# A hybrid attention and retention layer on one core: the last product as seven block products in a stage of its own, after both branches multiplied tile by tile

## The chip, the core and the metric

The kernel runs on one core of one Trainium2 chip. The metric is the device time of one execution in microseconds. Names used below: TensorE (PE, matmuls), its weight loads (PEld), VectorE (DVE), ScalarE (ACT), GpSimd (POOL), and SyncE (SP), the queue that issues every DMA of this kernel. PSUM is the memory that matmuls write their results to; a bank of it here holds a tile of 128 x 512.

## What is computed

One layer for 2048 frames of a new stream (the prompt) and 64 frames of running streams (the samples), with 1024 channels. Of the reference, cut to its end:

```
h = rmsnorm(x, norm_g) @ w_in        # one projection, split into columns
qa, ka, va, za, qb, kb, vb, zb, ga, gb = jnp.split(h, ...)
oa = diff_attention(qa, ka, va, ...) # branch A, 512 channels out
ob = retention(qb, kb, vb, ...)      # branch B, 512 channels out
...
def layer_output(x, oa, ob, za, zb, ga, gb, subln_g, lam_init, w_oa, w_ob, w_out):
    oa = (rmsnorm(oa, subln_g) * (1.0 - lam_init)).reshape(B, T, W_A) * jax.nn.silu(za)
    ob = rmsnorm(ob).reshape(B, T, W_B) * jax.nn.silu(zb)
    m = ga * (oa @ w_oa) + gb * (ob @ w_ob)
    return x + m @ w_out
```

`ga` and `gb` are sigmoids (with a bias per channel); `w_oa` and `w_ob` (in the kernel `w_o_diff` and `w_o_ret`) are 512 x 1024, `w_out` is 1024 x 1024. The change concerns `layer_output`. Everything is float32.

## The kernel before

**Products in parts.** Every float32 product is made of three matmuls on a high part (a cast by ACT) and a low part (the rest, mostly by DVE) of each operand: high by high, high by low, low by high. So each tile of an operand costs a cast and a subtraction before TensorE can use it.

**Order.** The program is written by tasks with priorities that a planner resumes one after the other along an estimated clock. A task takes a room in memory by `take` and hands it back by `give`; the number of rooms of each kind stands in `BUFS`. The order of TensorE, ACT and DVE is what the tasks write; SyncE's and POOL's orders are made from it afterwards by a scheduler. Each of these orders is fixed when the program is built: an instruction that waits holds back all that stand behind it on its engine.

**The closing stage.** The stages before it (projection, attention, retention) leave in DRAM the branch outputs `oaT`, `obT`, the raw gates of the branches `zaT`, `zbT` and the raw merge gates `gaT`, `gbT`, channels by tokens. `out_stream` (L1798) then goes through 8 groups of 264 columns, 256 tokens of the prompt and 8 of the samples each. For one group:

- `og_fin` (L1625) makes the eight operands of the branches (four per branch, 128 channels each): it loads `on` and `z`, multiplies on POOL (L1628), takes a sigmoid on ACT (L1631), multiplies on DVE (L1634), casts (L1642) and subtracts (L1645). The rooms for `on` and `z` are called "oz", those of the operands "og".
- `m_tile` (L1667) makes one tile of the merged product, 128 of the 1024 channels (`ct` counts them): for each branch four blocks of three matmuls 128x264 (L1685 to L1687) into a PSUM bank, `mm` for branch A and `s` for branch B, two banks of each. 192 matmuls for the eight tiles of a group.
- `gate` loads the two raw gates of the tile into rooms "gt" (8 of them) and takes the sigmoid (L1656); `m_fin` (L1696) multiplies each gate with its bank on DVE (L1704), adds the two on POOL (L1708), casts (L1714), subtracts (L1717), and copies the sample columns aside (`ms`, L1723).
- `y_tile` (L1727) multiplies 128 of the group's tokens with `w_out`: two halves of 512 channels, each 8 x 3 matmuls 128x512 (L1758 to L1760) into a bank `at`; `y_fin` adds x on DVE (L1791) and stores. Two of these per group, 96 matmuls. In the last group the tile of the 64 sample frames (L1752 to L1754, 32 matmuls) stands between the two.

So the branch product and the last product alternate, group by group. `load_wo` and `load_wout` load the weights and split them (`split_fin`). Loads are issued at L138, stores at L143, all on SyncE.

Of the kernel before, what the change touches and what calls it, by code (L numbers as in the profile page):

```python
# [35 lines left out]
        "oz": 11, "og": 16, "gt": 8, "wst": 4, "m": 16, "xt": 2, "yt": 2}  # L36
# [8 lines left out]
EARLY = 3  # L45
# [17 lines left out]
class Hybrid:  # L63
    def __init__(self, tc, ins, outs):
        self.tc = tc
        self.nc = tc.nc
        self.i = ins
        self.o = outs
        self.pe = self.act = self.dve = self.pool = self.dma = 0.0
        self.tasks = []  # L70
        self.seq = 0
        self.res = {k: Res(n) for k, n in BUFS.items()}
        self.res["row"] = Res(ROWS)
        self.live = {"z": 0, "w": 0, "r": 0}
        self.done = set()
# [79 lines left out]
    def scratch(self):  # L155
# [13 lines left out]
        self.obT = tc.dram_tile([4, 128, 8 * GW], F32, name="obT")  # L169

    def consts(self):
# [33 lines left out]
        nc.vector.tensor_scalar_mul(self.gsub, self.gsub, 0.8)  # L205
# [1201 lines left out]
    def ret_block(self, k, t0, r, first):  # L1407
# [88 lines left out]
        nc.vector.tensor_scalar(ms, ms, 1.0 / 128, EPS, op0=ALU.mult, op1=ALU.add)  # L1496
# [69 lines left out]
    def load_wo(self, q):  # L1566
        sl = slice(256 * q, 256 * q + 256)
        for br, name in enumerate(("w_o_diff", "w_o_ret")):
            for kt in range(4):
                h, l, slot = self.wo[br][kt]  # L1570
                yield from self.take("oz")
                s = self.sb(self.z3, [128, GW], "oz", "wst")[:, :256]
                t = self.ld(s, self.i[name][0, 128 * kt:128 * kt + 128, sl], 1 << 17)
                self.spawn(self.split_fin("oz", h[:, sl], l[:, sl], s, t, (kt + q) % 3 == 0, slot, q), 2)
                yield self.pe

    def load_wout(self):
        pool = self.z4
        for ct in range(8):
            h = pool.tile([128, 1024], F32R, tag=f"woh{ct}", name=f"woh{ct}")  # L1580
            l = pool.tile([128, 1024], F32R, tag=f"wol{ct}", name=f"wol{ct}")
            self.wout.append((h, l, {}))
        for nh in range(2):
            sl = slice(512 * nh, 512 * nh + 512)
            for ct in range(8):
                h, l, slot = self.wout[ct]
                k = 8 * nh + ct
                tag = ("xt", "xt", "yt", "yt")[k] if k < 4 else "wst"
                yield from self.take(tag)
                s = self.sb(pool, [128, 512], tag, "wst")  # L1590
                t = self.ld(s, self.i["w_out"][0, 128 * ct:128 * ct + 128, sl], 1 << 18)
                self.spawn(self.split_fin(tag, h[:, sl], l[:, sl], s, t + 600, False, slot, nh), 2)
                self.wout_left -= 1
                yield self.pe

    def out_prep(self):
        pa = self.z3
        for br, name in enumerate(("w_o_diff", "w_o_ret")):
            for kt in range(4):
                h, l = (pa.tile([128, 1024], F32R, tag=f"{name}{n}{kt}", name=f"{name}{n}{kt}") for n in "hl")  # L1600
                self.wo[br].append((h, l, {}))
        yield from self.load_wo(0)
        for g in range(8):
            gsl = slice(GW * g, GW * g + GW)
            for br, (oT, zT) in enumerate(((self.oaT, self.zaT), (self.obT, self.zbT))):
                for kt in range(4):
# [7 lines left out]
                    self.spawn(self.og_fin(on, z, t, og), 1)  # L1614
                    yield self.pe
            if g == 0:
                for ct in range(EARLY):
                    yield from self.take("oz", 2)
                    pair = [self.sb(pa, [128, GW], "oz", "gt") for _ in range(2)]
                    self.spawn(self.gate(ct, pair, "oz"), 1)  # L1620
                for q in range(1, 4):
                    yield from self.load_wo(q)
                yield lambda: self.wout_left == 0

    def og_fin(self, on, z, t, og):  # L1625
        nc = self.nc
        yield t
        nc.gpsimd.tensor_mul(on, on, z)  # L1628
        t = self.G(GW, self.pe)
        yield t  # L1630
        nc.scalar.activation(z, z, AF.Sigmoid)  # L1631
        t = self.A(GW, t)
        yield t
        nc.vector.tensor_mul(on, on, z)  # L1634
        t = self.V(GW + 100, t)
        self.give("oz", t)
        yield from self.take("og", 2)
        h = self.sb(self.z3, [128, GW], "og", "ogh", F32R)
        l = self.sb(self.z3, [128, GW], "og", "ogl", F32R)
# [10 lines left out]
    def gate(self, n, pair, tag):  # L1650
        g, ct = divmod(n, 8)
        for br, gT in enumerate((self.gaT, self.gbT)):
            t = self.ld(pair[br], gT[ct][:, GW * g:GW * g + GW], 1 << 17)
        yield t
        for br in range(2):
            self.nc.scalar.activation(pair[br], pair[br], AF.Sigmoid, bias=self.bg[:, br, ct:ct + 1])  # L1656
            t = self.A(GW, t, 123)
        self.gts[n] = (pair, t, tag)

    def gate_prep(self):  # L1660
        for n in range(EARLY, 64):
            yield from self.take("gt", 2)
            pair = [self.sb(self.z4, [128, GW], "gt") for _ in range(2)]
            self.spawn(self.gate(n, pair, "gt"), 0)
            yield self.pe

    def m_tile(self, g, ct, og):  # L1667
        nc = self.nc
        csl = slice(128 * ct, 128 * ct + 128)
        pss = []  # L1670
        for br, tag in ((0, "mm"), (1, "s")):
            yield from self.take(tag)
            ps = self.psum(tag)[:, :GW]
            for kt in range(4):
                wh, wl, tw = self.wo[br][kt]
# [336 lines left out]
```

## Time and profile before

| what | us |
|---|---|
| median of 3 runs (lowest, highest) | 1969.37 (1968.32, 1969.64) |
| profiled execution, its span | 1970.5 |
| TensorE busy from 1200 to 1588 us, of 388.0 | 388.0 |
| TensorE busy from 1588 us to the end, of 382.5 | 376.6 |
| DVE, ACT, POOL busy in the same 382.5 | 179.0, 129.1, 100.0 |
| branch matmuls of the first group: first start, then the first start of the second group | 1588.42, 1635.92 |

The profiled execution is one more run, taken with the profiler; its span is 1.1 us above the median of the timed ones. The profile gives the busy time of each engine, the idle time before each group of instructions with what ended it, and the start of each instruction. Matmuls overlap in their pipeline, so a row's duration is longer than the distance to the next start. From 1588 us on, the program is in the closing stage; DVE is busy for 47% of it, ACT for 34%, POOL for 26%.

### The profile page before, as it was taken

How to read it: one execution, taken by the hardware profiler on the slowest of the kernel's cores; microseconds unless marked ns; L12 is line 12 of the kernel's file. 1: busy time of each engine (PE TensorE's matmuls, PEld its weight loads, DVE VectorE, ACT ScalarE, POOL GpSimd, SP SyncE). 2: the span in 40 equal slices, each digit the busy share in tenths (PEclk: the TensorE clock that was granted, in tenths of full speed). 3: DMA queues.
4: the chain of work that ended last, by engine and by line, in shares of the span. 5: the costliest groups of instructions: out<-in, count | busy, mean ns of one | idle time of the engine just before them, and what ended most of it. 6: DMA issues, size and time to landing. Idle time of an engine off the chain costs nothing. (4 is left out here: it accounts for less than half of the span.)

```text
span 1970.5 us, 34013 instructions
## 1 busy us (share of the span) xinstructions
PE 1954.8 (99%) x12158; PEld 1753.9 (89%) x12158; DVE 1048.8 (53%) x2795; ACT 993.2 (50%) x2190; POOL 418.9 (21%) x387
## 2 busy tenths in 40 slices
PE   9999999999999999999999999999999999999999
PEld 7878999999988989999998888888888888888997
DVE  6553665536555236547757656635753356444433
ACT  6432776655544436436756666635654554333321
POOL 2310211212111121212112112112112434222210
PEclk9999999999999999999999999999999999999999
DMA  7647554336655656664352342553234666444432
GB/s 245 212 129 195 152 158 122 110 89 164 180 162 166 163 158 194 189 198 148 105 144 92 97 134 78 160 148 97 65 94 130 197 215 205 145 134 136 140 94 60
DMA packets 332429, 286.03 MB, mean 145 GB/s; under 512 B 65250, under 2 KB 296930, under 8 KB 332259
## 3 DMA queue, kind: packets, MB, share of 16 engines
q1 hardware_dynamic: 332258, 283.85, 49.0%
q8 instruction: 96, 1.57, 0.4%
q14 instruction: 75, 0.61, 0.1%
HBM read 187.22 MB, written 91.49 MB: 141 GB/s over the span
## 5 line engine op out<-in xcount | busy, mean ns | idle before, releaser
L516 PE MATMUL mm<-xh,wh 128*128 128x512 f32 (+2 forms) x1280 | 459.1, 359 | 0.0
L516 PE MATMUL mm<-xh,wl 128*128 128x512 f32 (+2 forms) x1280 | 452.3, 353 | 0.0
L516 PE MATMUL mm<-xl,wh 128*128 128x512 f32 (+2 forms) x1280 | 451.7, 353 | 0.0
L480 POOL TENSOR_TENSOR wl<-ws,wh 128x512 fp32r<-128x512 f32 x189 | 257.0, 1372 | 814.9 <-ACT wh L470 629.5
L516 PEld LDWEIGHTS mm<-xh,wl 128*128 128x128 f32 x1280 | 241.0, 188 | 31.6
L516 PEld LDWEIGHTS mm<-xh,wh 128*128 128x128 f32 x1280 | 241.3, 189 | 29.0 <-issue 0.2
L516 PEld LDWEIGHTS mm<-xl,wh 128*128 128x128 f32 x1280 | 241.6, 189 | 27.9
L516 PE MATMUL mm<-wh,xh 128*128 128x256 f32 (+1 forms) x824 | 258.4, 314 | 1.2 <-DVE tlo L753 1.0
L516 PE MATMUL mm<-wh,xl 128*128 128x256 f32 (+1 forms) x824 | 253.4, 308 | 0.0
L516 PE MATMUL mm<-wl,xh 128*128 128x256 f32 (+1 forms) x824 | 253.1, 307 | 0.1
L1119 DVE TENSOR_TENSOR atl<-at,ath 128x512 fp32r<-128x512 f32 (+1 forms) x144 | 93.8, 660 | 162.6 <-ACT ath L1117 162.6
L810 ACT COPY ev<-mm 128x512 f32<-128x512 f32 x140 | 71.5, 511 | 194.1 <-PE mm L516 166.0
L516 PEld LDWEIGHTS mm<-wh,xh 128*128 128x128 f32 x824 | 156.7, 190 | 10.9 <-DVE tlo L753 1.4
L516 PEld LDWEIGHTS mm<-wl,xh 128*128 128x128 f32 x824 | 156.9, 190 | 9.2 <-POOL wl L480 0.3
L516 PEld LDWEIGHTS mm<-wh,xl 128*128 128x128 f32 x824 | 156.7, 190 | 8.0
L1035 ACT ACTIVATE row<-row,a_mx 128x1024 f32<-128x1024 f32 (+7 forms) x160 | 153.9, 963 | 12.9 <-DVE a_mx L1015 12.6
L1005 DVE CUSTOM_DVE_ANT_0 row<-s,dfar 128x512 f32<-128x512 f32 (+2 forms) x192 | 118.6, 631 | 54.5 <-PE s L997 54.0
L470 ACT CAST wh<-ws 128x512 fp32r<-128x512 f32 x192 | 116.2, 619 | 44.8 <-PE mm L516 18.5
L1117 ACT CAST ath<-at 128x512 fp32r<-128x512 f32 (+1 forms) x144 | 79.0, 564 | 104.8 <-PE at L1104 97.4
L996 PE MATMUL s<-K,q 128*128 128x512 f32 (+3 forms) x320 | 118.7, 374 | 1.4 <-DVE a_acc L1005 1.4
L997 PE MATMUL s<-K,q 128*128 128x512 f32 (+3 forms) x320 | 115.2, 363 | 0.4 <-DMA q<-qT 0.4
L1057 DVE SCALAR_TENSOR_TENSOR row<-row,a_w 128x1024 f32<-128x1024 f32 (+4 forms) x96 | 103.6, 1086 | 14.4 <-ACT row L1054 14.1
(238 smaller groups left out, 4036.1 us busy)
## 6 DMA issues: line engine op xcount, KB each, us to landing
ws<-in_w_in_dram SPq DMA_DIRECT2D x192, 256.0 KB, 3.0
q<-qT SPq DMA_DIRECT2D x128, 128.0 KB, 3.1
V<-vN SPq DMA_DIRECT2D x24, 512.0 KB, 5.5
K<-kT SPq DMA_DIRECT2D x48, 256.0 KB, 4.2
gt<-gaT SPq DMA_DIRECT2D x64, 132.0 KB, 2.1
gt<-gbT SPq DMA_DIRECT2D x64, 132.0 KB, 2.2
xt<-in_x_prompt_dram SPq DMA_DIRECT2D x16, 512.0 KB, 6.1
kn<-in_cache_k_T_dram SPq DMA_DIRECT2D x32, 256.0 KB, 3.7
```

What stands on the lines that cost most here:

```text
L470: self.nc.scalar.copy(h, st)
L480: self.nc.gpsimd.tensor_sub(l, st, h.bitcast(F32))
L516: nc.tensor.matmul(ps, p, q, start=c == 0 and i == 0, stop=c == KC - 1 and i == 2)
L810: nc.scalar.copy(ev, ps)
L996: nc.tensor.matmul(ps, q1s, kk, start=True, stop=False)
L997: nc.tensor.matmul(ps, q2s, kk, start=False, stop=True)
L1005: nc.vector.tensor_tensor_reduce(out=units[k0 // 1024][:, k0 % 1024:k0 % 1024 + n], in0=ps, in1=tab, scale=-SLOPES[h], scalar=3.0e38, op0= ...
L1035: nc.scalar.activation(u, u, AF.Exp, bias=mx, scale=-1.0, accum_out=lp[:, k:k + 1])
L1057: nc.vector.scalar_tensor_tensor(out=u0, in0=u0, scalar=w[:, 0:1], in1=u1, op0=ALU.mult, op1=ALU.add)
L1117: nc.scalar.copy(ah[:, :w], at[:, :w])
L1119: nc.vector.tensor_sub(al[:, :w], at[:, :w], ah[:, :w].bitcast(F32))
```

## The change

The change takes the closing stage apart into two.

**The branch stage.** All 64 tiles `(g, ct)` of the merged product come first, without the last product between. The gates become `Tanh` of half the argument (the bias is halved, and the factor 0.5 goes into the constants of the branches' norms), and one DVE instruction per branch (`scalar_tensor_tensor`) adds one and multiplies with the bank. `og_fin` uses `Silu` on ACT and one product on POOL. POOL's sum is not split any more but stored to a new DRAM array `mT`, and only then the rooms of the gate come free; there are 10 rooms "gt". Every third set of four operands lies in rooms "ob" in another memory pool. The weights of the branches lie in two halves of 512 channels; the rooms of the first half are called "wa".

**The last stage.** The tokens of a group (two halves of 128), the merged channels (two halves of 512) and the output channels (two halves) give 2 x 2 blocks: a11, a21, a22, a12 of the merged product (channel half by token half; each 128x4x128 in memory) and 11, 12, 21, 22 of `w_out`. `y_group` makes the four output blocks of a group from seven block products (P1 to P7) of 4 x 3 matmuls 128x512 each, with sums and differences of the operands (s1 to s4 and t1 to t4):

| product | operands | PSUM bank | taken from the bank behind it |
|---|---|---|---|
| P1 | a11, 11 | mm, fresh | copy on ACT, room "u" |
| P2 | a12, 21 | s, fresh | DVE adds P1 + x: first output |
| P6 | s2, t2 | mm, on top of P1 | copy on ACT, room "u" |
| P5 | s1, t1 | at, fresh | copy on ACT, room "u" |
| P7 | s3, t3 | mm, on top | DVE adds the copy of P5 + x: second output |
| P3 | s4, 22 | at, on top of P5 | DVE adds the copy of P6 + x: third output |
| P4 | a22, t4 | mm, on top | DVE adds x: fourth output |

Here s1 = a21 + a22, s2 = s1 - a11 (DVE), s4 = a12 - s2, s3 = a11 - a21 (POOL), and each operand of a product is cast on ACT (L1801) and split on DVE (L1808). POOL adds x to the copies (L1704). `t1` to `t4` are differences of the blocks of `w_out`; `b_prep` makes them during the branch stage (DVE, L1706) and splits them (DVE, L1766); eight of their sixteen tiles have no room then: they wait, unsplit, until the first half of the branch weights has been used for the last time (tile ct = 3 of group 7), and are split into its rooms "wa" (`b_late`).

`y_open` waits until all merged tiles are stored, closes the branch operands' pool and opens in its place the rooms "ac" (parts of operands), "u" and "xt" (blocks of x). The operands of P1 and P2 of the first group go to other rooms ("st"), so these two products don't wait for that. The samples (`y_sample`, 40 matmuls, since the block 12 of `w_out` isn't kept and its product is made from the blocks 11 and t1) stand in the last group, ahead of P6.

Loads are issued at L140 and stores at L145 in the new kernel, still all on SyncE. The core of the diff:

```diff
-        "oz": 11, "og": 16, "gt": 8, "wst": 4, "m": 16, "xt": 2, "yt": 2}
+        "oz": 11, "og": 16, "ob": 8, "gt": 10, "wa": 16, "st": 13, "ac": 16, "u": 9, "xt": 10}
...
+BLOCKS = ("11", "21", "22", "t1", "t2", "t3", "t4")
+PAIRS = {"P1": ("a11", "11"), "P6": ("s2", "t2"), "P2": ("a12", "21"), "P7": ("s3", "t3"),
+         "P5": ("s1", "t1"), "P4": ("a22", "t4"), "P3": ("s4", "22")}
...
     def og_fin(self, on, z, t, og, third):
...
+        nc.scalar.activation(z, z, AF.Silu)
...
         nc.gpsimd.tensor_mul(on, on, z)
...
+    def gates(self):
+        for n in range(64):
+            g, ct = divmod(n, 8)
+            yield from self.take("gt", 2)
+            pair = [self.sb(self.z3p, [128, GW], "gt") for _ in range(2)]
+            for gt, gT in zip(pair, (self.gaT, self.gbT)):
+                t = self.ld(gt, gT[ct][:, GW * g:GW * g + GW], 1 << 17)
+            self.spawn(self.gate(n, ct, pair, t), 0)
+            yield self.pe
...
-            self.nc.scalar.activation(pair[br], pair[br], AF.Sigmoid, bias=self.bg[:, br, ct:ct + 1])
+            self.nc.scalar.activation(pair[br], pair[br], AF.Tanh, scale=0.5, bias=self.bg[:, br, ct:ct + 1])
...
     def m_fin(self, g, ct, pss):
...
-            nc.vector.tensor_mul(gs[br], ps, gs[br])
+            nc.vector.scalar_tensor_tensor(out=gs[br], in0=gs[br], scalar=1.0, in1=ps, op0=ALU.add, op1=ALU.mult)
...
         nc.gpsimd.tensor_add(gs[0], gs[0], gs[1])
         t = self.G(GW, t)
-        yield from self.take("m", 2)
...
+        self.give("gt", t)
+        yield t
+        t = self.st(self.mT[ct][:, GW * g:GW * g + GW], gs[0], 1 << 17)
+        self.give("gt", t)
...
+    def y_group(self):
...
+        for g in range(8):
+            seq += [(g, p) for p in ("P1", "P2", "P6", "P5", "P7", "P3", "P4")]
+        bank = {"P1": "a", "P6": "a", "P7": "a", "P4": "a", "P2": "b", "P5": "c", "P3": "c"}
+        tags = {"a": "mm", "b": "s", "c": "at"}
...
+            fresh = p in ("P1", "P2", "P5")
...
+            for c in range(4):
...
+                for m, (u, v) in enumerate(((ah[:, c], wh), (ah[:, c], wl), (al[:, c], wh))):
+                    nc.tensor.matmul(q[b], u, v, start=fresh and c == 0 and m == 0, stop=c == 3 and m == 2,
+                                     skip_group_check=True)
...
     def out_stream(self):
...
         for g in range(8):
             og = []
             for ct in range(8):
                 yield from self.m_tile(g, ct, og)
-            for tt in range(2):
...
+        self.spawn(self.y_open(), 0)
+        yield from self.y_group()
+
+    def y_open(self):
+        yield lambda: self.live["m"] == 0
+        self.z3.close()
+        self.z6 = self.es.enter_context(self.tc.tile_pool(name="p3y", bufs=1, side="right"))
+        for k in ("ac", "u", "xt"):
+            self.give(k, self.pe, BUFS[k])
+        self.spawn(self.y_x(), 0)
```

What this moves, in the built orders. In these rows stand the line, the operation, and the tile written, then those read; the number behind a name tells tiles of one name apart. First TensorE before, where the first group's branch product ends and its last product begins:

```order
L1685 MATMUL s_18713<-ogh_18082,w_o_reth3_17795 128x264
L1686 MATMUL s_18713<-ogl_18083,w_o_reth3_17795 128x264
L1687 MATMUL s_18713<-ogh_18082,w_o_retl3_17796 128x264
L1758 MATMUL at_18738<-woh0_18384,mh_18461 128x512
L1759 MATMUL at_18738<-wol0_18385,mh_18461 128x512
L1760 MATMUL at_18738<-woh0_18384,ml_18462 128x512
```

In the new kernel the change from 264 to 512 wide matmuls stands once, behind the last group's branch product. The rows are TensorE's there: the last of branch B, then P1 (`bh11`, `bl11` are the parts of block 11, `ah`, `al` those of a11):

```order
L1670 MATMUL s_21370<-ogh_21050,woh13_17816 128x264
L1671 MATMUL s_21370<-ogl_21051,woh13_17816 128x264
L1672 MATMUL s_21370<-ogh_21050,wol13_17817 128x264
L1882 MATMUL mm_21385<-bh11_18393,ah_19819 128x512
L1882 MATMUL mm_21385<-bl11_18394,ah_19819 128x512
L1882 MATMUL mm_21385<-bh11_18393,al_19820 128x512
```

So seven alternations between the two widths are gone, and P1 follows the branch stage at once. Next DVE of the new kernel at the same place, from the second product of the last merged tile on (`gt` is a gate, `a` a block or block sum, `al` a low part, `u` an output):

```order
L1690 SCALAR_TENSOR_TENSOR gt_21259<-gt_21259,s_21370 128x264
L1706 TENSOR_TENSOR a_21435<-a_21349,a_21351 128x512
L1706 TENSOR_TENSOR a_21437<-a_21435,a_21347 128x512
L1808 TENSOR_TENSOR al_21450<-a_21437,ah_21449 128x512
L1932 TENSOR_TENSOR u_21426<-s_21427,u_21426 128x512
L1808 TENSOR_TENSOR al_21453<-a_21435,ah_21452 128x512
L1808 TENSOR_TENSOR al_21465<-a_21349,ah_21464 128x512
```

Here the low part of s1 (`al_21453`, for P5) stands behind the addition that ends P2's output (L1932). DVE also has such a place at the boundary between two groups of the branch stage, the second and the third. There the rows begin with the last tile's second product, and then come a split of t3 and the low parts of the next group's operands:

```order
L1690 SCALAR_TENSOR_TENSOR gt_19052<-gt_19052,s_19170 128x264
L1766 TENSOR_TENSOR blt3_18404<-wst_18837,bht3_18403 128x512
L1628 TENSOR_TENSOR ogl_19175<-on_18805,ogh_19174 128x264
L1628 TENSOR_TENSOR ogl_19178<-on_18827,ogh_19177 128x264
L1628 TENSOR_TENSOR ogl_19181<-on_18860,ogh_19180 128x264
L1628 TENSOR_TENSOR ogl_19184<-on_18893,ogh_19183 128x264
```

These low parts are written behind the last tile of the old group, since their rooms are freed by it. Last SyncE, before, at the load of a new group's operands; `gt<-gaT` is the load of a gate:

```order
L138 DMA gt_21488<-gaT_69 128x264
L138 DMA gt_21489<-gbT_70 128x264
L138 DMA gt_21582<-gaT_69 128x264
L138 DMA gt_21583<-gbT_70 128x264
L138 DMA on_21560<-oaT_71 128x264
L138 DMA z_21570<-zaT_67 128x264
```

And SyncE in the new kernel, in the last third of the branch stage; `mT<-gt` is the store of a merged tile:

```order
L145 DMA mT_73<-gt_20467 128x264
L140 DMA gt_20681<-gaT_69 128x264
L140 DMA gt_20682<-gbT_70 128x264
L145 DMA mT_73<-gt_20541 128x264
L140 DMA gt_20731<-gaT_69 128x264
L140 DMA z_20761<-zbT_68 128x264
L140 DMA gt_20732<-gbT_70 128x264
```

Here `gt_20682` gets the room of `gt_20467`, and waits for the landing of the store two rows above it; `gt_20732` in the same way for the store of `gt_20541`. The store of a merged tile, which did not exist before, stands between the loads.

485 lines of the change are left out of this document (324 added, 161 removed).

## The prediction

> **What bounds the kernel now.** I read the page of the profile first, then the table of TensorE's waits from 1588 us to the end, then the timeline of TensorE.
>
> ```profile
> span 1970.5 us, 34013 instructions
> PE 1954.8 (99%) x12158; PEld 1753.9 (89%) x12158; DVE 1048.8 (53%) x2795; ACT 993.2 (50%) x2190; POOL 418.9 (21%) x387
> PEclk9999999999999999999999999999999999999999
> ...
> PE at L1758 <- DVE oyt L1791: 0.8, 1, 0.8
> ```
>
> The page shows TensorE busy for 99% of the span at full granted clock, and every other engine near half. In the waits (engine and line, what was waited for, us, times, longest) the largest entry of the whole closing stage is 0.8 us. So TensorE's stream of matmuls is the path, and what the change is worth is the matmuls it removes, less the waits that it adds.
>
> The built order of TensorE is the same in both kernels up to the first matmul of the closing stage (L1685 before). The stage therefore starts at the same time, and only its length is in question. The timeline (start, duration, instruction) gives its ends and the two rates inside it:
>
> ```profile
> 1588.42 0.28 PE L1685 MATMUL mm<-ogh,w_o_diffh 128*128 128x264 f32 x1
> ...
> 1683.26 0.28 PE L1685 MATMUL mm<-ogh,w_o_diffh 128*128 128x264 f32 x1
> ...
> 1706.54 0.28 PE L1687 MATMUL s<-ogh,w_o_retl 128*128 128x264 f32 x1
> ...
> 1955.53 0.39 PE L1758 MATMUL at<-woh,mh 128*128 128x512 f32 x1
> ...
> 1966.39 0.40 PE L1760 MATMUL at<-woh,ml 128*128 128x512 f32 x1
> ```
>
> Durations overlap, so starts are what counts. From 1683.26 to 1706.54 stand the 192 branch matmuls of one group: 23.28 / 191 = 0.1219 us each. From 1955.53 to 1966.39 stand the last 48 of the last product: 10.86 / 47 = 0.2311 us each. The stage runs from 1588.42 to 1966.39 + 0.23 = 1966.62, that is **378.2 us**. It issues 8 x 192 = 1536 branch matmuls (187.2 us) and 800 of the last product, 768 for the prompt and 32 for the samples (184.9 us). The sum is 372.1, so 6.1 us are gaps. A gap looks like this, a pair of PSUM banks not yet emptied between two halves of a group:
>
> ```profile
> 1671.54 0.39 PE L1760 MATMUL at<-woh,ml 128*128 128x512 f32 x1
> 1672.02 0.50 PE L1758 MATMUL at<-woh,mh 128*128 128x512 f32 x1
> ```
>
> The start comes 0.48 after the one before, 0.25 more than the rate. After the last matmul come one add and one store, up to 1970.5. The new kernel ends the same way, so that tail stays.
>
> **What the change removes and adds on TensorE.** Seven block products of 4 x 3 = 12 matmuls each replace 96 matmuls per group by 84: 672 in place of 768. The samples take 40 in place of 32, since their second half uses two blocks where one weight stood. At 0.2311 us that is 155.3 + 9.2 us. Without any gap the stage would be 187.2 + 155.3 + 9.2 = **351.7 us**, 26.5 less than now. Whether the new operands (other tiles, same 128x512) keep the rate is not shown; the nearest rows of that shape bound it from below:
>
> ```profile
> 1576.17 0.39 PE L516 MATMUL mm<-xh,wh 128*128 128x512 f32 x1
> ...
> 1588.18 0.40 PE L516 MATMUL mm<-xh,wl 128*128 128x512 f32 x1
> ```
>
> These are 54 matmuls in a row: 12.01 / 53 = 0.2266 us. With it the 712 would take 3.2 us less. I take 0.2311, the row of the same product, and keep 3.2 us as the lower end.
>
> **The work beside it.** Durations that I use, from the groups of the closing stage by form (count, busy us, mean ns), and one from the whole run (POOL, 128x512):
>
> ```profile
> L1656 ACT ACTIVATE gt<-gt,bg 128x264 f32<-128x264 f32 x122 | 57.6, 509 | 12.1 <-DMA gt<-gbT 5.6 <-DMA gt<-gaT 5.3 <-DVE ms L1723 0.8
> L1708 POOL TENSOR_TENSOR gt<-gt 128x264 f32<-128x264 f32 x64 | 53.5, 837 | 152.8 <-DVE gt L1704 78.0 <-DVE ms L1723 72.0 <-DMA wst<-in_w_out_dram 2.7
> L1704 DVE TENSOR_TENSOR gt<-s,gt 128x264 f32<-128x264 f32 x64 | 27.5, 430 | 35.2 <-PE s L1687 35.0
> L1645 DVE TENSOR_TENSOR ogl<-on,ogh 128x264 fp32r<-128x264 f32 x56 | 25.7, 513 | 0.5 <-ACT ogh L1642 0.5
> L1791 DVE TENSOR_TENSOR oyt<-at,oxt 128x512 f32<-128x512 f32 x32 | 22.0, 689 | 57.0 <-PE at L1760 57.0
> L1561 DVE TENSOR_TENSOR wol<-wst,woh 128x512 fp32r<-128x512 f32 x16 | 10.9, 688 | 2.6 <-ACT woh L1554 2.6
> L1554 ACT CAST woh<-wst 128x512 fp32r<-128x512 f32 x16 | 9.7, 617 | 2.7 <-DMA wst<-in_w_out_dram 2.5
> ...
> L480 POOL TENSOR_TENSOR wl<-ws,wh 128x512 fp32r<-128x512 f32 x189 | 257.0, 1372 | 814.9 <-ACT wh L470 629.5 <-PE mm L516 69.2 <-PE mm L512 47.1
> ```
>
> In the new last stage a group lasts 84 x 0.2311 = 19.4 us. DVE does 13 passes of 512 in it (two block sums, seven low parts, four outputs): 13 x 0.689 = 9.0 us. ACT does seven casts and three copies: 10 x 0.617 = 6.2. POOL does two sums and three additions of x: 5 x 1.372 = 6.9. All three stay under half of 19.4, so this work is hidden behind the products. Every bank is emptied while another product of 12 x 0.2311 = 2.8 us runs, against a copy of 0.6 or an add of 0.7.
>
> In the new branch stage a tile (g, ct) takes 24 x 0.1219 = 2.93 us, where it had 5.8 with the last product between. Per tile DVE does 2 x 0.430 + 0.513 = 1.4 us, POOL one gate sum and one product, 1.7. ACT does two gates and, by the rows of 264 above, two more passes of about 0.4 to 0.5: 1.9. Tanh and Silu have no row here. The same engine's Sigmoid with a bias per partition takes 0.509; ACT stays off the path up to (2.93 - 0.9) / 2 = 1.0 us per gate, twice the row. I take the row. The adds of one into a gate (one pass with PSUM) I put at the 0.430 of the product that they replace.
>
> One place is tight. Rooms of a branch's old operands come free 12 matmuls before the group's end, and the next group needs the new ones 24 x 0.1219 = 2.93 us later. At the boundary of the second and third group VectorE has to do the last tile's second product (not before 1.6 us, when it ends), a split of 0.69 and then four low parts of 0.51. The first is ready at 1.6 + 0.43 + 0.69 + 0.51 = 3.2, the fourth at 4.8 against a need at 2.93 + 1.10 = 4.0. That costs **0.8 us** once. The other six boundaries have no split there; I put 0.2 each for a late semaphore, **1.2 us**.
>
> **SyncE's queue.** It now carries, per tile of the branch stage, one store of the merged tile and two gate loads, and two more loads for most tiles. What an issue and a landing take is in the timeline of SyncE, in the DMA tables for the two windows 1601 to 1647 and 1693 to 1855 us, and in the one for the whole run (count, KB, median us to landing), with the traffic from the table of stretches:
>
> ```profile
> 1708.69 0.38 SPq L138 DMA_DIRECT2D on<-oaT  x1
> ...
> 1710.12 0.38 SPq L138 DMA_DIRECT2D z<-zbT  x1
> 1601.00:1624.00 23.00, 22.69 (x139) 19.52 (x137) 16.66 (x46) 11.93 (x26) 9.19 (x10) 1.00 0.77 247
> 1693.00:1739.00 46.00, 45.92 (x290) 41.33 (x289) 21.05 (x60) 16.01 (x40) 12.66 (x17) 1.00 0.47 143
> out_y_prompt_dram<-oyt SPq DMA_DIRECT2D x4, 256.0 KB, 3.0
> gt<-gaT SPq DMA_DIRECT2D x6, 132.0 KB, 3.6
> ...
> out_y_prompt_dram<-oyt SPq DMA_DIRECT2D x12, 256.0 KB, 2.0
> oxt<-in_x_prompt_dram SPq DMA_DIRECT2D x12, 256.0 KB, 3.3
> gt<-gaT SPq DMA_DIRECT2D x30, 132.0 KB, 2.1
> ...
> gbT<-ev SPq DMA_DIRECT2D x16, 128.0 KB, 3.4
> zaT<-ev SPq DMA_DIRECT2D x8, 128.0 KB, 1.7
> ```
>
> Four issues in a row come every (1710.12 - 1708.69) / 3 = 0.48 us. Five per tile are 2.4 of its 2.93 us, so SyncE has half a microsecond left to wait. In the built order the second gate load of a tile, in about the last third of the stage, waits for the store that was issued just ahead of it. There SyncE needs, per tile, the landing of that store plus 0.48 us, and it keeps pace while a store lands within 2.93 - 0.48 = **2.45 us**. For 132 KB the rows say 1.7 to 3.4; the 256 KB ones 2.0 at 143 GB/s and 3.0 at about 240. Where the pattern is strictest (the 11 tiles before the last five) only three DMAs of 132 to 135 KB run per tile, 3 x 0.135 / 2.93 = 138 GB/s, so I take 2.0 there, and SyncE keeps pace. For the seven earlier tiles of that kind the traffic is 4 to 5 DMAs, 185 to 230 GB/s; with 3.0 us SyncE falls 0.55 behind per tile, 3.9 in all. Behind a store and a load hang 5 tiles of gates, 14.6 us, of which 0.9 (products) + 0.8 (sum) + 2.5 (store) + 0.5 + 3.6 (load) + 1.0 (gates) = 9.3 and some 1.5 for semaphores are used. The slack is about 4 us, the same size as the lag. I take **2.0 us** of waiting, with 0 and 10 as ends.
>
> **From one stage to the other.** The first copy out of PSUM (u, on ACT) takes a room in memory that the branch stage's tiles held, and waits until the last merged tile is stored. From the end of the last branch matmul: 0.15 (drain, an estimate from the 0.40 us duration against 0.23 spacing) + 0.43 + 0.84 + 2.5 = 3.9 us. P1 and P2 cover 5.6 us. The x blocks are loaded into those rooms too: 3.9 + 3.3 = 7.2, POOL's add 8.6, P2's output on DVE 9.3, and behind it in DVE's order the low part of s1, 10.0. P5 wants that low part with its third matmul, at 8.3 + 0.5 = 8.8. So about 1.2 us of wait, and with semaphores **2.0 us**; between 0 and, with the x load at 5 and the store at 3.4, 4.5. For the rest of the stage I put **0.5 us**.
>
> [...]
>
> **The sum.** 351.7 + 0.8 + 1.2 + 2.0 + 2.0 + 0.5 = 358.2 us for the stage, 20.0 less than 378.2. The profiled execution spans 1970.5 us, 1.1 above the median of the runs; 1970.5 - 20.0 - 1.1 = **1949.4 us**.
>
> **The rivals.**
> - **SyncE paces the gates.** Stores land at the 3.4 us of the slowest 128 KB row in all 18 tiles: each takes 3.4 + 0.48 - 2.93 = 0.95 more, 17.1 less 4 of slack, 13 us of waits in place of 2. That gives 1960. For it: traffic doubles, the row exists. Against: 138 GB/s in most of these tiles.
> - **The same queue, further on: slower than before.** The gain is gone when these waits reach 22 us: 18 x (L + 0.48 - 2.93) - 4 = 22, so from a landing of L = 3.9 us. At 4.3 us it is 1949.4 + 27.3 = 1976.7. No group of 128 KB stores is that slow.
> - **Products wait for their banks.** Each of 56 products shows the 0.25 + 0.1 us of the gap quoted above: 19.6 us, so that nothing is won: 1969. Against it: 2.8 us of cover per bank, and copies of 0.6.
> - **No gaps at all**, and the faster rate: down to 1969.4 - 26.5 - 3.2 = 1939.7.
>
> **How the numbers follow.** Forecast 0.65; SyncE paces 0.20; products wait 0.07; slower by the queue 0.05; better than 1943 0.03. A measurement of this kernel can tell about 0.2%, 4 us, from no change. Faster by more than that: all but the slow case and the full price of the third rival, 0.91; within 0.2%: 0.04; slower 0.05. The range is 1943 (no gaps at 0.2311) to 1961, which takes in the first rival.
>
> **What would show it.** In the profile after: the merged stage ends near 1588 + 187 + 4 = 1779 us and P1's first matmul follows it; matmuls of a group of the last stage at 0.231 spacing, 19.4 us a group; TensorE's waits on gates (its PSUM banks) under 4 us in all; DVE in the last stage under half busy. Wrong would be: gate loads that land late with ACT waiting for them in the groups 5 to 7, a gap at the stage's start over 4.5 us, or a gap at each product.

## The result, and the profile after

The changed kernel takes **1957.41 us** (median of 4 runs, 1955.6 to 1963.03) against 1969.51 before (4 runs, 1968.32 to 1974.08). The ratio is 0.9939, with a 95% interval of 0.9922 to 0.9957: 8.5 to 15.4 us faster. The forecast was 1949.4 with a range of 1943 to 1961. The direction and the range held; the gain is 12.1 us where 20.0 were forecast. The first rival (SyncE paces the gates, 1960) is the nearer of the two.

The head of the page of the changed kernel, and TensorE's waits (us, times, longest) from the stage's start to the end:

```profile
span 1955.4 us, 34054 instructions
PE 1936.0 (99%) x12070; PEld 1740.5 (89%) x12070; DVE 1068.5 (55%) x2642; ACT 1021.7 (52%) x2220; POOL 476.0 (24%) x427
...
PE s L1671 <- DVE ogl L1628: 2.8, 5, 1.5
PE at L1882 <- DVE al L1808: 2.1, 1, 2.1
PE s L1670 <- ACT ogh L1625: 1.4, 2, 0.8
PE mm L1670 <- DVE gt L1690: 1.1, 1, 1.1
```

Before, the largest entry of this part was 0.8 us. Now there are 5.3 us in the branch stage (first, third and fourth row: parts of the branches' operands and a bank) and 2.1 at the start of the last stage. Three starts from TensorE's timeline give the lengths of the stages (first branch matmul, P1, the last product):

```profile
1586.05 0.29 PE L1670 MATMUL mm<-ogh,woq 128*128 128x264 f32 x1
...
1784.42 0.39 PE L1882 MATMUL mm<-bh,ah 128*128 128x512 f32 x1
...
1951.36 0.39 PE L1882 MATMUL mm<-wot,al 128*128 128x512 f32 x1
```

The branch stage takes 1784.42 - 1586.05 = **198.4 us**, forecast 187.2 + 4.0 = 191.2. The last stage takes 1951.36 + 0.23 - 1784.42 = **167.2 us**, forecast 155.3 + 9.2 + 2.5 = 167.0. Together 365.5 in place of 378.2: 12.7 less. (The stage also begins 2.4 us earlier than in the execution before, at 1586.05 for 1588.42. Nothing was changed ahead of it, and in the runs below it begins between 1585.4 and 1588.4.) So the missing 7 us are in the branch stage. Its groups 1 to 7 (counted from 0) and the last stage, in the table of stretches (length, busy time of PE, PEld, DVE, ACT and POOL, granted clock, DMA share, GB/s):

```profile
1609.41:1635.20 25.79, 24.32 (x195) 23.62 (x193) 19.15 (x33) 15.00 (x36) 15.39 (x17) 1.00 0.85 262
1635.20:1662.85 27.65, 25.40 (x194) 24.99 (x193) 19.08 (x35) 17.11 (x42) 15.89 (x19) 0.94 0.85 262
1662.85:1686.89 24.04, 23.77 (x194) 23.44 (x193) 15.97 (x32) 14.57 (x35) 13.04 (x17) 1.00 0.90 265
1686.89:1714.18 27.29, 25.98 (x194) 25.13 (x193) 11.98 (x27) 17.02 (x43) 13.37 (x18) 0.94 0.85 248
1714.18:1737.61 23.43, 23.43 (x194) 23.43 (x193) 10.04 (x24) 12.32 (x30) 11.88 (x17) 1.00 0.77 222
1737.61:1760.96 23.35, 23.35 (x195) 23.35 (x194) 10.53 (x27) 11.03 (x28) 8.20 (x11) 1.00 0.56 163
1760.96:1784.42 23.46, 23.46 (x195) 23.46 (x193) 14.20 (x27) 11.08 (x22) 7.09 (x8) 1.00 0.56 162
1784.42:1951.59 167.17, 165.07 (x714) 132.30 (x712) 85.31 (x110) 44.26 (x80) 56.24 (x41) 1.00 0.51 151
```

A group of 192 matmuls at 0.1219 us lasts 23.4. Groups 5 to 7 run at that rate; groups 1 to 4 lose 2.4, 4.3, 0.6 and 3.9 us, in the stretch where DMA is at 0.85 to 0.90 of its engines. In groups 2 and 4 the granted clock falls too, to 0.94 on the mean. What the loss of group 4 looks like stands in the timelines at its start (SyncE, ACT and PE, in order of time):

```profile
1683.51 0.38 SPq L140 DMA_DIRECT2D gt<-gaT  x1
1683.95 0.48 SPq L140 DMA_DIRECT2D gt<-gbT  x1
...
1687.12 0.52 ACT L1646 ACTIVATE gt<-gt,bg 128x264 f32<-128x264 f32 x1 [1.43 <-DMA gt<-gaT]
1688.23 0.51 ACT L1646 ACTIVATE gt<-gt,bg 128x264 f32<-128x264 f32 x1 [0.59 <-DMA gt<-gbT]
1688.65 1.33 ACT L1625 CAST ogh<-on 128x264 fp32r<-128x264 f32 x4
...
1689.10 0.39 PE L1670 MATMUL s<-ogh,woq 128*128 128x264 f32 x1 [0.59 <-ACT ogh L1625]
```

TensorE waits for a cast. The cast's engine is idle, but in its fixed order two gates stand ahead of it, and these wait for loads that SyncE issued only 3.4 and 2.9 us before the group began. So a gate that lands late holds back an operand that has nothing to do with it.

The largest loss, at the start of group 2, looks otherwise (ACT, DVE and PE, in order of time):

```profile
1634.70 1.13 ACT L1763 CAST bht<-wst 128x512 fp32r<-128x512 f32 x2
1635.34 2.44 DVE L1766 TENSOR_TENSOR blt<-wst,bht 128x512 fp32r<-128x512 f32 x2 [2.37 <-ACT bht L1763]
1635.73 0.98 ACT L1646 ACTIVATE gt<-gt,bg 128x264 f32<-128x264 f32 x2
1636.62 0.60 ACT L1763 CAST bht<-wst 128x512 fp32r<-128x512 f32 x1
1637.13 2.60 ACT L1625 CAST ogh<-on 128x264 fp32r<-128x264 f32 x8
1637.59 0.39 PE L1670 MATMUL s<-ogh,woq 128*128 128x264 f32 x1 [0.77 <-ACT ogh L1625]
1638.38 0.68 DVE L1766 TENSOR_TENSOR blt<-wst,bht 128x512 fp32r<-128x512 f32 x1
1638.98 2.37 DVE L1628 TENSOR_TENSOR ogl<-on,ogh 128x264 fp32r<-128x264 f32 x5
1639.45 0.39 PE L1671 MATMUL s<-ogl,woq 128*128 128x264 f32 x1 [1.47 <-DVE ogl L1628]
```

ScalarE waits for nothing here. Ahead of the casts in its order stand three casts of blocks of `w_out` and two gates, and VectorE has three splits of blocks ahead of the low parts. So two different things delay the operands: late gates at group 4, split work at group 2.

### The profile page after: what moved, and what is told of

The parts are those of the page before. It is cut to its first block, busy times and chain, and to the rows that moved or that the text cites. A ratio compares the mean times of both kernels' runs of the same rounds, so it can differ in the third digit from the quotient of the medians.

```text
span 1955.4 us, 34054 instructions
## 1 busy us (share of the span) xinstructions
PE 1936.0 (99%) x12070; PEld 1740.5 (89%) x12070; DVE 1068.5 (55%) x2642; ACT 1021.7 (52%) x2220; POOL 476.0 (24%) x427
## 4 chain that ended last, share of the span: by engine, by line
PE 91%; DVE 3%; DMA 3%; ACT 1%; issue 1%; SPq 1%; POOL 1%; ACTq 0%; DVEq 0%; POOLq 0%
PE mm L520 53%; PE mm L1882 4%; PE s L1000 3%; PE s L1001 3%; PE at L1108 3%; PE at L1882 2%; PE pv L1088 2%; PE pv L1087 2%; PE pv L1086 2%; PE mm L1670 1%; PE mm L1672 1%; PE mm L1671 1%; PE s L1671 1%; PE s L1672 1%; PE s L1670 1%; PE s L1882 1%
## 5 line engine op out<-in xcount | busy, mean ns | idle before, releaser
L814 ACT COPY ev<-mm 128x512 f32<-128x512 f32 x140 | 71.4, 510 | 191.2 <-PE mm L520 177.9
```

The source lines that it names most:

```text
L814: nc.scalar.copy(ev, ps)
```

## The experiments

Theories: **split work** (differences and splits of `w_out` on VectorE and ScalarE delay the parts of the operands), **SyncE** (its queue makes gates and operands late, by the number of issues or by waiting for landed stores), **conversion** (the parts of the operands have too little time at a boundary, whatever else happens). Every run was executed once, sum_apart_mo4_lo six times. Branch stage means from the first 264 wide matmul to P1.

| run | branch stage, us | whole, us |
|---|---|---|
| changed kernel | 198.4 | 1957.41 (median) |
| again | 196.5 | 1957.40 |
| loads_only | 198.7 | 1958.83 |
| splits_only | 206.5 | 1967.99 |
| late_blocks | 205.4 | 1965.00 |
| stores_act | 199.4 | 1956.66 |
| gates_later | 197.3 | 1955.58 |
| gt8 | 204.0 | 1966.76 |
| sum_apart | 201.1 | 1964.60 |
| gates_one_load | 221.6 | 1984.78 |
| sum_apart_mo4_lo | 200.4 | 1960.04 (median of 6) |
| old_operands | 195.7 | 1957.49 |
| lo_first | 198.9 | 1954.88 |

**again.** The changed kernel once more. 

> The changed kernel once more, unchanged, to see how far its branch stage (198.4 us) and the waits in it repeat. If the waits are set by the fixed orders of the queues, the stage is within 1 us of 198.4, with the waits at the same group boundaries; if they come from chance in the landing of DMAs, it differs by several us.

 It gave 196.5, with losses in groups 1 to 4 once more, though in other shares (1.2, 2.9, 4.3 and 0.4 us): the place repeats, the size of the whole stage within 2 us in these two executions. The times of the changed kernel's five executions spread over 7.4 us (1955.6 to 1963.03), so a single time below says little unless it lies well outside that range; only gates_one_load does, and the next, splits_only, is 5.0 us above its upper end.

**loads_only and splits_only.** Each drops one side of the blocks' preparation for three of the four row blocks: loads_only the differences and splits, splits_only the loads.

```diff
+        skip = c > 0 and self.q_end is None     # loads_only, in b_split and for the differences
+        if not skip:
             self.nc.scalar.copy(h, s)
...
+            if c == 0:                          # splits_only, in b_raw
                 t = self.ld(raw[k], w[128 * r:128 * r + 128, n:n + 512], 1 << 18)
+            else:
+                raw[k] = self.raw0[k]
```

> All 16 loads of blocks of the last weight stay, and so do SyncE's and TensorE's orders; the differences and splits of three of the four row blocks in the branch stage are left out (the seven block weights of row block 0 stand for the others, so the last product's values are not the reference's). The branch stage is 198.4 us in the changed kernel, from the first 264 wide matmul to P1, against 187.2 at the plain rate. Theory 'split work': VectorE and ScalarE spend the time at the group boundaries on differences and splits, so the next operands are cast and split late; then the boundaries of the first three groups close and the stage is 189 to 193 us, and only the wait at the fourth boundary (where no split stands) stays. Theory 'SyncE': the queue of DMAs can't keep up with loads, stores and blocks together, so gates and operands land late; then the stage stays at 196 to 199 us.

> The other half: 12 of the 16 block loads (256 KB each) are left out, while all differences and splits stay and work on the blocks of row block 0 (so the last product's values are not the reference's). Theory 'split work': the stage stays at 195 to 199 us. Theory 'SyncE': with 12 DMAs fewer among the first four groups' some 220, gates and operands land earlier and the stage is 189 to 193 us.

Without three quarters of that work the stage is 198.7, so **split work is not the only cause**. Groups 1 and 2 lose 1.1 and 1.8 us in place of 2.4 and 4.3, but group 3 loses 7.3 in place of 0.6: at its start TensorE waits 3.2 us for a cast, and ahead of that cast two gates wait for their loads (0.98 and 1.12 us). With 12 loads fewer the stage is not shorter either; it is 206.5. SyncE then waited 34.6 us for landed stores, where the changed kernel waits 21.7. Theory SyncE, as far as it counts issues, expected the opposite. Full DMA engines are not the whole reason either: in splits_only groups 2 to 4 have DMA at 0.71 to 0.75, and lose 2.8, 2.6 and 4.8 us.

**stores_act, late_blocks.** Two other ways to relieve SyncE in the first groups.

```diff
-        t = self.st(self.mT[ct][:, GW * g:GW * g + GW], gs[0], 1 << 17)
+        self.nc.scalar.dma_start(self.mT[ct][:, GW * g:GW * g + GW], gs[0])
...
-                yield lambda: self.b_left < 13
...
+        yield lambda: len(self.mt[3]) == 8      # late_blocks, at the head of b_prep
```

> The 64 stores of merged tiles are issued by ScalarE in place of SyncE. Theory 'SyncE': one issue in five leaves its queue, 64 x 0.48 = 31 us of issue time, and the waits at the boundaries go: 189 to 193 us for the branch stage. Theory 'split work': no change at the first three boundaries, 195 to 199 us. On the other side, ScalarE's order then holds a store that waits for POOL's sum; if that delays the gates behind it, the stage gets longer than 199 us.

> The loads, differences and splits of the blocks of the last weight begin only once group 3 is merged, in the groups 4 to 7 that had no waits. Both theories expect the first boundaries to close. 'Split work': the waits move to the later boundaries where the splits now stand, so the branch stage is 192 to 196 us. 'SyncE': the later groups have time left in the queue (all operands of a group are loaded by then, and no gap stood there), so 188 to 192 us. If the whole preparation doesn't fit into four groups, P1 starts late by several us and the time is no better than the changed kernel's.

199.4 and 205.4. Neither met what the theories expected; stores_act is just over the 199 that its expectation gives for stores that delay the gates in ScalarE's order, but the difference is smaller than that between the changed kernel and again. In both, SyncE's loads waited longer for landed stores than before (45.5 and 33.6 us). A reading that fits: when there is less ahead of a gate's load in the queue, it comes to its head sooner and waits there for its room, with everything behind it. But the sum of these waits doesn't tell the length of the stage: stores_act has the larger one and the shorter stage.

**gt8, sum_apart, gates_one_load.** The rooms of the gates, and what a load has to wait for.

```diff
+        "gt": 8                                          # gt8
...
+        nc.gpsimd.tensor_add(mo, gs[0], gs[1])           # sum_apart, "gt": 8, "mo": 2
+        self.give("gt", t, 2)
...
+            gt = self.sb(self.z3p, [128, 2, GW], "gt")   # gates_one_load, "gt": 5
+            t = self.ld(gt, self.gT[ct][:, :, GW * g:GW * g + GW], 1 << 18)
```

> 8 rooms for the gates instead of 10, one tile less in flight. Theory 'landing': the ring of a gate's rooms (load, gate, product, sum, store landed) is what is tight; it loses 2.9 us of slack per turn, and the branch stage gets longer than 205 us, with TensorE waiting for banks. Theory 'issue' or 'split work': the ring is not what is tight; 197 to 201 us.

> POOL writes the merged tile into a room of its own (2 rooms), and a gate's rooms come free at POOL's sum; gates have 8 rooms for 10, so the memory is the same, and no load of a gate waits for the landing of a store. Theory 'landing': SyncE's 21.7 us of waits for landed stores hold back the loads behind them, gates come late, and ScalarE's casts of the next group's operands stand behind the late gates; without those waits the branch stage is 188 to 193 us. Theory 'issue': SyncE's queue is simply full (0.48 us per DMA, five per tile, and the blocks), whatever it waits for: the stage stays at 196 to 200 us. If 4 pairs of gates are too few, TensorE waits for its banks on the gates, and the stage is over 200 us.

> The raw gates of both branches lie side by side in DRAM and come in one load per tile (264 KB) in place of two; the traffic is the same, SyncE issues 64 DMAs fewer, and a tile's pair of gates is one room (5 of them, the same memory), free when the merged tile's store has landed. Theory 'issue': in the groups 1 to 4 SyncE issued 45 to 48 DMAs per group, 22 to 23 us at 0.48 each, of 23.4 us that a group should last; with 8 fewer per group it is 18 to 19 us, and the branch stage shrinks from 196.5 to 198.4 us to 188 to 192 us. Theory 'landing': each load now waits for the landing of a store, in every tile, and holds back what stands behind it; the stage is 197 us or longer. A ring of rooms that is too tight would show as TensorE waiting for banks on VectorE's gates.

gt8 gives 204.0, with 7.9 us of waits for banks: the ring of rooms counts, with about 6 us for two rooms of the ten. gates_one_load differs most: 64 issues fewer, the same traffic, and the stage is 221.6. SyncE's waits in that stage, first in the changed kernel, then in this one:

```profile
SPq L140 <- DMA mT<-gt: 21.7, 18, 3.2
```

```profile
SPq L140 <- DMA mT<-gt: 58.4, 36, 3.8
```

So **fewer issues alone gain nothing**. What costs the 23 us isn't separated here: the loads wait longer at the head of the queue, but the ring is tighter too, since a pair of gates is one room that is held until the store has landed, where in the changed kernel one of a pair's two rooms comes free at POOL's sum. sum_apart took the waits for landed stores away and gave 201.1. Two waits stood in their place: SyncE's loads waited 28.5 us for POOL's sums, and POOL waited for one of its two rooms (POOL's waits, sum_apart):

```profile
POOL mo L1696 <- DMA mT<-mo: 25.9, 20, 4.2
```

**sum_apart_mo4_lo.** Four such rooms, paid for with two rooms of raw operands, and the order of lo_first (below).

```diff
-        "oz": 11, ... "gt": 10
+        "oz": 9, ... "gt": 8, "mo": 4
```

> The merged tile in a room of its own as in sum_apart, but with 4 rooms for it in place of 2 (there POOL's sum waited 25.9 us for the landing of earlier stores), 8 rooms for gates, and 9 rooms in place of 11 for the branches' raw operands, which pays for it; and the order of lo_first in the last stage. Theory 'ring': in the changed kernel a gate's room is held from the issue of its load to the landing of the store, 12.5 to 13.9 us to the store's issue in the groups 1 to 3 and 3.1 more to its landing, 16 to 17 us, against 5 tiles x 2.93 = 14.6 us. Here it is held to POOL's sum only, some 10 us against 4 x 2.93 = 11.7, and a room of the sum some 9 us against 11.7. So the branch stage falls to 188 to 193 us, and the whole to 1945 to 1951. Theory 'SyncE is full' (45 to 48 DMAs per group at 0.48 us): the stage stays at 196 to 200 and the whole at 1952 to 1956. If the raw operands now come late, TensorE waits for parts of operands at the group boundaries and the stage is over 200 us.

200.4 us, and 1960.04 for the whole (ratio to the kernel before 0.9949, 0.9935 to 0.9962): **no better than the changed kernel**. No gate's load waits for the landing of a merged tile any more, and POOL's waits for rooms fell from 25.9 to 4.6 us over the stage, but groups 1 to 3 still lose 2.5 to 4.6 us each. So those landings are not the one cause. The ring as such isn't ruled out: the gates have 8 rooms here, as in gt8 (204.0), and SyncE's loads wait 27.7 us for POOL's sums.

**gates_later, old_operands.** Who suffers from the late gates?

```diff
     def gate(self, n, ct, pair, t):
-        yield t
+        yield t + 2500                          # gates_later
...
+        if k < 8:                               # old_operands, in og_fin
             nc.scalar.copy(h, on)
```

> The planner counts a gate's load as landed 2.5 us later, so in ScalarE's order the gates stand behind more of the casts; nothing else is changed. Theory 'casts behind gates': TensorE's waits for the parts of the next operands (4.2 us, and the lower clock that follows) come from casts that stand behind gates which nobody needs yet; with the gates moved back the stage is 190 to 194 us. If the gates are then late themselves, TensorE waits for banks (DVE's product with the gate) and the stage stays over 197 us.

> From the second group on, the branch matmuls use the parts of the first group's operands: the 48 casts and 48 low parts of the groups 1 to 7 are left out, so the values are not the reference's. All loads, Silu, POOL's products, gates, stores, blocks and SyncE's pace stay, and TensorE's order too. Theory 'conversion at the boundary': the parts of branch B's next operands can only be written when the old ones' rooms are free, 24 matmuls (2.93 us) before they are used; what stands beside them on ScalarE and VectorE (late gates, differences and splits) makes them late, and this is nearly all of the 9.3 to 11.2 us. Without the conversion the branch stage is 187.5 to 190 us, and TensorE's waits for banks stay under 1.5 us in all. Theory 'late gates': gates come late on their own account in the groups 1 to 3, and if no cast is there to be held back, TensorE waits for its banks (VectorE's product with the gate) instead: 193 to 198 us.

With the gates behind the casts, the waits for parts of operands fall to 2.2 us, but TensorE waits 4.3 us for banks, and the stage is 197.3. Without any conversion after the first group it is 195.7, and TensorE's waits in the stage are these (old_operands, whole table):

```profile
PE mm L1676 <- DVE gt L1696: 6.3, 8, 1.4
```

Seven of the eight stand in groups 1 to 3. So **conversion is not the only limit: the gates are late on their own account**, and where no cast is held back by them, the banks are. In groups 1 to 3 the second gate of a tile was ready only after the tile's last matmul had started in 14 of 24 tiles here, and in 6 of 24 in the changed kernel (rows of ACT and PE). Late gates are not the only limit either: in sum_apart_mo4_lo that holds for 2 of 24 tiles, and yet TensorE waited 5.1 us for parts of operands. The two limits lie close together, and taking one away shows the other.

**lo_first.** The stage transition.

```diff
+        if (g, p) == (0, "P2"):
+            yield lambda: (0, "s1") in self.ya
```

> Only VectorE's order changes at one place: in the first group of the last stage the low part of s1 stands ahead of the addition that ends P2's output. If that addition (which waits through POOL, the block of x and its room for the last merged store) is what held P5 for 2.1 to 2.3 us, the wait goes to under 0.5 us, and the last stage gets some 2 us shorter than the 167.2 of the changed kernel (P1's first matmul to the last one's end); the branch stage stays at 196 to 199. If P5 really waits for the load of its own block, nothing changes.

The wait of 2.1 us is gone (TensorE has no wait left in the last stage), and that stage takes 1949.06 + 0.23 - 1784.48 = 164.8 us, the plain 155.3 + 9.2 + 0.3. In gates_later the order that was built anew has the low parts ahead of that addition too, and the wait is absent there as well. The whole is 1954.88 in one run, 0.7 us under the fastest of the changed kernel; with a spread of 7.4 us that can't be told from no gain.

## Why the prediction was right, and where it was not

- **The bound and what is removed: right.** 712 matmuls in place of 800; a group of the last stage has a period of 19.47 us (1863.60 - 1844.13, the starts of the same matmul one group on), forecast 19.4; over 84 matmuls that is 0.2318 each, for 0.2311.
- **Products wait for banks: no.** Not one wait at a bank of the last stage in the table.
- **From one stage to the other: right in size and cause.** 2.0 forecast, 2.1 in the table, at the third matmul of P5, and lo_first took it away.
- **Work beside the products: hidden, though mis-sized.** DVE is busy for 85.31 of 167.17 us, 51%, where I had 9.0 of 19.4 (46%), so the sign "under half" was missed: passes with two inputs in memory took 0.88 us on the mean, where I had put 0.689 (below).
- **SyncE's queue: the step that failed.** "Five per tile are 2.4 of its 2.93 us, so SyncE has half a microsecond left to wait." In groups 1 to 3 SyncE issued 140 DMAs for 24 tiles, 5.8 per tile, since the blocks of `w_out` and the operands of a group ahead come in the same stretch; the queue waited 16.7 of those 77.5 us besides. The gate loads landed in 3.3 to 3.5 us there, against 2.1 to 2.5 later. The turn of a gate's rooms, 9.3 us and an estimate of mine of 1.5 for semaphores in the forecast, has two more terms there: POOL began a tile's sum 1.5 us behind the second product, and SyncE issued the store 2.0 us behind the sum (medians over the 24 tiles; longest 6.5 and 5.4). From the first gate's issue to the landing of the store it was 16.4 us, against 14.6 for five tiles, and in that there is time in which a ready gate waits for its product. The DMA tables for groups 1 to 3 and 5 to 7 (count, KB, median us to landing):

```profile
gt<-gaT SPq DMA_DIRECT2D x25, 132.0 KB, 3.3
gt<-gbT SPq DMA_DIRECT2D x25, 132.0 KB, 3.5
mT<-gt SPq DMA_DIRECT2D x25, 132.0 KB, 3.1
...
mT<-gt SPq DMA_DIRECT2D x24, 132.0 KB, 2.2
gt<-gbT SPq DMA_DIRECT2D x21, 132.0 KB, 2.1
gt<-gaT SPq DMA_DIRECT2D x20, 132.0 KB, 2.5
```

- I looked for the trouble where the built order shows a load right behind the store it waits for. That pattern is real: 21.4 of the 21.7 us of such waits lie in groups 5 to 7, as told. It costs nothing there: groups 5 to 7 run at the plain rate, with 88 DMAs in 70 us. The 2.0 us that I put for it belong to groups 1 to 4, and to more.
- **The boundaries: mis-sized.** 0.8 + 1.2 forecast, the 1.2 an estimate of mine for late semaphores that no run shows apart. With the queue's term 4.0 in all, 11.2 measured: 7.1 are gaps between matmuls and 4.1 a wider spacing behind them, most of it the lower clock: the sum has no term for that, and in two falls of 3.41 us a matmul came every 0.22 us in place of 0.1219, which makes 2 x 3.41 x (1 - 0.1219 / 0.22) = 3.0 us. I took ScalarE as free at a boundary; in its order stand gates, which wait for DMAs, and casts of blocks. The boundary that I priced at 0.8 us is the start of group 2. TensorE waited 0.77 and 1.47 us there: the sum has one split of 0.69 us, but two more stood ahead of the last tile's products, and those two took 2.44 us.
- **The rivals.** "SyncE paces the gates" came near in time (1960), and late gates are a part of it; but its mechanism (stores landing in 3.4 us in 18 late tiles) is not what happened: stores landed in 2.2 us at the median in groups 5 to 7, and the waits for them cost nothing. That its time is the nearer one is luck.

What stays open: what makes the gates late in groups 1 to 4, and how much of the 7 us is theirs. For SyncE's queue speaks the place (in the changed kernel, the stretch with most DMAs), and that the runs with more waits in it for landed stores were mostly slower (gates_one_load, splits_only, late_blocks; not stores_act). Against a plain count of DMAs speak late_blocks and gates_one_load: 36 to 45 DMAs a group and losses of up to 4.0 us in groups 1 to 4 of the one, 19 to 33 a group and losses of 4.0 to 7.0 us in groups 5 to 7 of the other. POOL's order is a rival that no run tested: a merged tile's sum stands there behind products for the next operands, and these wait for loads in their turn (POOL, group 1; the Silu named there had itself waited 4.8 us for its load):

```profile
1622.21 0.75 POOL L1615 TENSOR_TENSOR on<-on,z 128x264 f32<-128x264 f32 x1 [4.06 <-ACT z L1612]
1622.92 1.21 POOL L1694 TENSOR_TENSOR gt<-gt 128x264 f32<-128x264 f32 x1
```

No run that relieved one thing shortened the stage by more than the kernel repeats. Each order is built anew, and the wait moves on. Stores on another queue together with a room of their own for the sums would separate it further; that wasn't tried, nor were more rooms for gates.

## What to carry to other kernels

When two interleaved stages are pulled apart, one of them may have been the cover for the other's loads and conversions, which fits what is seen here: 96 matmuls of the last product stood between two groups, and without them three rings (gates, operands, stores) have to turn in 2.93 us per tile. Count every DMA of the stretch in which the stage is densest, not the average per tile, and look in each fixed order for what stands behind an instruction that waits for a DMA. A relief of such a queue is worth trying, but one that makes a load wait at the queue's head and holds its room for longer can cost more than it saves (gates_one_load: 64 issues fewer, 23 us longer). Time the unchanged kernel several times first: here it spread over 7.4 us, more than most of the differences that were looked for.

## What was not expected of the hardware

**The clock fell after short waits.** At the start of group 2 TensorE waited 0.77 and 1.47 us with one matmul between (rows above); 1.4 us later the granted clock was 0.50 for 3.41 us, and a matmul came every 0.22 us in place of 0.1219. At the start of group 4, from 1692.02 us on, it was 0.50 for 3.41 us too, with 0.22 us from matmul to matmul. The same pair of waits in again, 1.08 and 1.35 us there, left the clock at 1.00 up to 1641.27 us (first its two rows, then the stretches of 3.4 us before and behind the start of the first fall in the changed kernel, then again's at its pair of waits; the clock is the third number from the right, and x counts the rows that touch a stretch):

```profile
1637.43 0.39 PE L1670 MATMUL s<-ogh,woq 128*128 128x264 f32 x1 [1.08 <-ACT ogh L1625]
1639.18 0.39 PE L1671 MATMUL s<-ogl,woq 128*128 128x264 f32 x1 [1.35 <-DVE ogl L1628]
...
1637.40:1640.82 3.42, 1.76 (x12) 1.56 (x13) 3.42 (x9) 3.42 (x11) 0.64 (x1) 1.00 0.79 238
1640.82:1644.23 3.41, 3.41 (x17) 3.41 (x17) 3.41 (x8) 2.21 (x6) 1.48 (x3) 0.50 0.72 231
...
1634.45:1637.86 3.41, 2.30 (x17) 1.88 (x15) 2.62 (x4) 3.41 (x9) 1.91 (x2) 1.00 0.83 234
1637.86:1641.27 3.41, 2.09 (x17) 2.10 (x18) 3.41 (x8) 3.41 (x11) 1.24 (x2) 1.00 0.80 232
```

So such a pair of waits came with the lower clock in one execution of this kernel and without it in another. What decides between the two was not shown.

**VectorE beside POOL.** In the last stage passes of 512 with both inputs in memory took 0.88 us on the mean, those with one input from PSUM 0.69 (groups of DVE, the stretch from 1785 us):

```profile
L1808 DVE TENSOR_TENSOR al<-a,ah 128x512 fp32r<-128x512 f32 x54 | 46.3, 880 | 26.1 <-ACT ah L1801 18.9 <-PE at L1882 4.5 <-DMA a<-mT 2.6
...
L1932 DVE TENSOR_TENSOR u<-at,u 128x512 f32<-128x512 f32 x8 | 5.5, 689 | 11.2 <-PE at L1882 11.2
```

The mean hides two sizes, by the rows of DVE and POOL from 1586 us on. Of the passes of L1808, the 35 with no POOL row beside them took 0.67 to 0.69 us each, and the 21 that began while POOL was in an instruction 1.20 on the mean, up to 1.79. The low parts of L1628 (128x264) took 0.42 us alone, 0.42 too in the ten cases where POOL began in their course, and 0.85 on the mean where POOL was running when they began. Passes with one input from PSUM stayed at 0.68 to 0.69 us beside POOL. What makes the passes with both inputs in memory longer there was not shown. The forecast's 0.513 for a low part is such a mean as well: the 35 passes of L1645 without POOL beside them took 0.42 us, and those that began while POOL was running up to 1.00. No run here varied POOL's work alone.
